# One layer on one core: the fourth and eighth token block's scaling ahead of the memory norms, norm weights on another queue, pooling work spread in the fill

## The chip, the core and the metric

One NeuronCore of a Trainium2 chip runs the whole program. Its engines work side by side and wait for each other through semaphores: TensorE (PE) for matmuls and transposes, VectorE (DVE), ScalarE (ACT), GpSimd (POOL), and SyncE (SP), which here only issues DMAs. The metric is the device time of one execution in microseconds, lower is better.

## The reference

One mixer layer over 1024 tokens of width 1024, in float32:

```python
h = rmsnorm(x, norm_g)
proj = h @ w_in            # pool_v 256 | pool_gate 256 | q, k, v, gate 512 each | mem_q 256 | mem_gate 256
a = pool_mixer(pool_v)     # causal means over 2, 4, 8, 16 tokens minus the token, a 64x64 map per group, a scale
b = stick_breaking_attention(q, k, v)   # 8 heads of 64, strictly causal: sigmoid breaks and their running products
c = memory_attention(mem_q, rmsnorm(mem, mem_norm_g) @ w_mem_kv)  # 4 heads, softmax over 256 memory tokens, q and k normed
out = x + concat(a * silu(pool_gate), b * silu(gate), c * silu(mem_gate)) @ w_out
```

## The kernel before

Every float32 product is made of three faster ones: each operand is split into a high part (`hh`, `wh_*`, written by ACT) and the rest (`hl`, `wl_*`, by DVE or POOL), and PE adds high x high, high x low and low x high. A step of a projection unit `u_*` is these three matmuls of 512 columns for one of eight slices of the width; a unit makes 128 channels in two token halves, so it has 16 steps.

*The beginning.* The two blocks of memory tokens `m[0]`, `m[1]` and the eight of `x` are loaded by SP, with the norm weights as rows of `grow` between them. PE transposes the memory (`m_tr`, tile `tm`) and the norm weights (`gains`, tile `gps`, copied to `gcol` as columns, by which `m_evac` scales what it writes to `mh` and `ml`). The memory's keys and values are accumulated in two banks `kv0`, `kv1` (`kv_step`). A token block is normed in steps of the class `Norm`: `square` (ACT), `root`, `newton` (two 128x1 operations on DVE, three where a column `col` is asked for), `scale` (128x1024, in place, on DVE or POOL). `h_step(th, k)` then transposes slice k of four blocks (tile `tx`) and writes `hh` and `hl`: blocks x0 to x3 are the first half (`th` 0), x4 to x7 the second. The tile x67 holds x6 and x7. `mq_high` and `mq_low` split the weights of the memory queries, whose two units (`u_mq`) run eight slices alternating with `h_step`s; in that loop over k lie also the norms of x4 to x7, the memory's own norms (`mn`, whose result `rm` scales the keys and values) and `kv_evac` (ACT writes `kv` times `rm` to `kvs`). Here the order on DVE, ACT and POOL is that of the code (a manual schedule).

*The attentions.* A list of main steps (scores, transposes, products with the values) and a list `fill` of projection steps are woven by `weave`: it emits fill steps until its model of time says that what the next main step needs is ready. A `Step(pe, fn, occ, lat, needs, gives)` gives that model PE's time, the engines' time and the latency behind it. In the memory attention (`mem_main`) `tr` transposes the weights of 256 tokens to `ta_m`, from which ACT makes `ah_m` and DVE `al_m`, and `av` multiplies both by the memory's values. In the four stick-breaking attentions (two heads each) `ta`, `ah`, `al`, `av` play the same parts; the breaks lie in `be`.

*The pooling.* `pool_parts(r, ...)` gives for channel half r a projection unit `u_pv`, and a list `po[r]`: loading the small map, window sums (`us`, `ps2`, on DVE), means (DVE, then `ph` by ACT and `pl` by POOL), and last two products `py` that are multiplied into the gate `gp`. All but the products cost PE nothing. The lists are inserted into the fill of the last attention at given positions. `ph0` lies in the buffer qb0 and `pl0` in KA0.

*The end.* The mixed channels are multiplied by `w_out` (`oA`, `oS`) in a scheme with fewer products; its weights are loaded into the buffers qa0, qb0, KA0 and others (`quads`, `load_b`), split by `split_b` to `bs`, and the first product (A11) begins behind the last gate's unit `u_mg1`.

Of the kernel before, what the change touches and what calls it, by code (L numbers as in the profile page):

```python
# [14 lines left out]
P = 128  # L15
# [5 lines left out]
HD = 64  # L21
# [4 lines left out]
def layer_kernel(  # L26
# [15 lines left out]
    nc = tc.nc  # L42
# [42 lines left out]
    grow = pool.tile([P, P], F32, tag="pw", name="grow")[0:20, :]  # L85
# [262 lines left out]
    nc.sync.dma_start(grow[8:16, :], mem_norm_g[0].rearrange("(k p) -> k p", p=P))
    nc.sync.dma_start(mt[1][:], mem[0][P : 2 * P, :])
    nc.sync.dma_start(grow[0:8, :], norm_g[0].rearrange("(k p) -> k p", p=P))  # L350
    nc.sync.dma_start(grow[16:18, :], pool_scale[0].rearrange("(k p) -> k p", p=P))
    nc.sync.dma_start(grow[18:19, 0:HD], q_norm_g[0:1, :])
    nc.sync.dma_start(grow[19:20, 0:HD], k_norm_g[0:1, :])
    mn = [Norm(mt[i][:], f"m{i}") for i in range(2)]
    xn = [Norm(xt[i][:], f"x{i}") for i in range(NT)]
    gcol = const.tile([P, 24], F32, name="gcol")
# [8 lines left out]
    def m_tr(i):  # L365
        for kk in range(4):
            for j in range(2):
                k = 2 * kk + j
                nc.tensor.transpose(tm[kk][:, j * M + i * P : j * M + (i + 1) * P], mt[i][:, k * P : (k + 1) * P], ident[:])

    def gains():
        gps = ps("tr", "gps")
        nc.tensor.transpose(gps[:, 0:18], grow[0:18, :], ident[0:18, 0:18])
        nc.tensor.transpose(gps[0:HD, 32:52], grow[:, 0:HD], ident[0:20, 0:20])
        nc.vector.tensor_copy(gcol[:, 0:18], gps[:, 0:18])
# [80 lines left out]
    def kv_newton():  # L456
# [13 lines left out]
        fill=1.0,  # L470
# [102 lines left out]
    def mem_main(mq, ys):  # L573
# [50 lines left out]
        steps = []  # L624
        n = len(items)
        for t in range(n + 4):
            if t < n:
                steps.append(Step(0.44, lambda it=items[t]: qk(it), 1.5, 2.5, [("q", t - 3)], ("q", t)))
            if 0 <= t - 3 < n:
                steps.append(Step(0.43, lambda it=items[t - 3]: tr(it), 0.7 if t < n else 2.2, 2.4, [("q", t - 3)], ("t", t - 3)))  # L630
            if 0 <= t - 4 < n:
                steps.append(Step(0.44, lambda it=items[t - 4]: av(it), 0.3, 0.0, [("t", t - 4)]))
        return steps
# [176 lines left out]
    mn[0].square()  # L810
    mn[1].square()
    m_tr(0)
    gains()
    m_tr(1)
    warm(kvp[1], 4)
    m_evac(0)
    kv_split(0)
# [18 lines left out]
    xn[2].root(True)  # L836
    kv_step(3)
    xn[2].newton()
    xn[3].square()
    xn[3].root(True)  # L840
    xn[2].scale(nc.vector)
    raw_mq = [load_raw(w_in_v[:, :, 2560 + pr * P : 2560 + (pr + 1) * P], f"mq{pr}", early_raw[4 + pr]) for pr in range(2)]
    for i in range(4, 8):
        nc.sync.dma_start(xt[i][:], xv[i * P : (i + 1) * P, :])
# [9 lines left out]
    def mq_low(pr, c, eng):  # L854
        wh, wl = w_mq[pr]
        eng.tensor_tensor(wl[:, c], raw_mq[pr][:, c], f(wh[:, c]), op=ALU.subtract)

    mq_high(0, wc[0])
    mq_low(0, wc[0], nc.gpsimd)
    mq_high(0, wc[1])  # L860
    mq_high(1, wc[0])
    mq_low(1, wc[0], nc.gpsimd)
# [27 lines left out]
    for k in range(KD):  # L890
        half[0, 0][k][1]()
        half[1, 0][k][1]()
        if k + 3 < KD:
            h_step(0, k + 3)
        if k >= 5:
            h_step(1, k - 5)
        if k == 1:
            for i in range(2):
                mn[i].root()
        if k == 3:  # L900
            for i in range(2):
                mn[i].newton(col=rm[:, i : i + 1])
        if k <= 3:
            xn[4 + k].newton()
        if k < 2:
            xn[6 + k].square()
            xn[6 + k].root()
        if k <= 3:
            xn[4 + k].scale(nc.gpsimd if k < 2 else nc.vector)
        if k == 3:  # L910
            u_q[0].weights()
        if k == 4:
            kv_evac()

    plan = {-1:((0, 0), (0, 1), (0, 2)), 0: ((0, 3), (0, 4)), 1: ((1, 0), (1, 1),(1, 2)), 2: ((1, 3),), 3: ((1, 4),)}
# [44 lines left out]
    gm, u_gm = zip(*[gate_unit(2816 + pr * P, f"mg{pr}", "be", lambda pr=pr: y_mem[pr], (("pj", "pj"), ("tr", "av"))[pr]) for pr in range(2)])  # L960
    u_pv, po = zip(*[pool_parts(r, gp[r]) for r in range(2)])
    weave(attn(2), chain([u_q[3], u_k[3], u_v[3]]+[u_g[3]], u_pv[1]), 4, 1.0)
    fill = chain([u_pv[1], u_gp[1], u_pv[0], u_gp[0]]+[u_gm[0]], u_gm[1])
    for r, at in ((0, 46), (1, 22)):
        for n, st in enumerate(po[r][:-2]):
            fill.insert(at + 2 * n, st)
    at = 70 + len(po[0]) + len(po[1]) - 4
    fill[at:at] = po[0][-2:-1]
    fill[at + 6 : at + 6] = po[0][-1:]
    at = 44 + len(po[1]) - 2  # L970
    fill[at:at] = po[1][-2:-1]
# [106 lines left out]
    w1 = split_b("B11", b1)  # L1078
    t1 = quads("KA0")
    load_b(t1, 0, 1)  # L1080
    run(u_gm[1].steps[:8])
    split_a("A11", raw[0, 0])
    s3 = quads("V0")
    tt("S3r", s3, raw[0, 0], raw[1, 0], ALU.subtract)
# [93 lines left out]
```

## Time and profile before

| | us |
|---|---|
| median of 3 runs | 524.44 (523.58 to 524.48) |
| the profiled execution | 524.41 |
| its span, first to last instruction | 522.6 |
| PE busy | 509.8 |
| DVE busy | 392.4 |
| ACT busy | 289.8 |
| POOL busy | 166.4 |

In a row of the view in order of time stand the start and the duration in us, the engine, the line, the operation, the tile written and the tiles read (without their numbers), the shapes and the count; in brackets how long the engine had been idle and what ended that. SPq rows are DMAs being issued. Overlapping rows of one engine are pipelined. In the view of waits stand the total in us, how often, and the longest.

### The profile page before, as it was taken

To read this page: it belongs to the slowest core of one execution; us is meant where nothing else is said; L and a number is where in the kernel's file an instruction comes from. 1 tells how busy PE (TensorE), PEld (TensorE's weight loads), DVE (VectorE), ACT (ScalarE), POOL (GpSimd) and SP (SyncE) were. 2 spreads that over 40 slices of the span, in tenths; PEclk is the share of its full clock that TensorE was granted. 3 is DMA by queue.
4 is the path that set the end of the run, shared out by engine and by line. 5 is a ranking of instruction groups with operands and counts; after the bars stand their busy time and mean duration, and the time that the engine had idled before them with its cause. 6 is when DMAs were issued, how large, how long until landed. Compare 5 with 4: busy or idle time off the path is not lost.

```text
span 522.6 us, 7475 instructions
## 1 busy us (share of the span) xinstructions
PE 509.8 (98%) x2724; PEld 429.3 (82%) x2724; DVE 392.4 (75%) x635; ACT 289.8 (55%) x562; POOL 166.4 (32%) x190
## 2 busy tenths in 40 slices
PE   7889999999999999999999999999999999999997
PEld 6678888888888888888888888888788888888886
DVE  4776777777487876877748776748988769999973
ACT  6887657677555654645545655445535539452400
POOL 4480335244212112202201220122436910044890
PEclk9999999999999999999999999999999999999999
DMA  8911021310111131033101122110110525513033
GB/s 298 349 44 41 7 76 43 80 41 0 41 40 42 42 80 41 0 82 80 42 1 40 41 69 54 40 42 7 35 41 0 162 64 180 163 39 135 26 118 124
DMA packets 37244, 37.25 MB, mean 71 GB/s; under 512 B 1990, under 2 KB 26840, under 8 KB 37208
## 3 DMA queue, kind: packets, MB, share of 16 engines
q1 hardware_dynamic: 37208, 36.78, 22.6%
q8 instruction: 21, 0.34, 0.3%
q14 instruction: 15, 0.12, 0.1%
HBM read 28.39 MB, written 4.19 MB: 62 GB/s over the span
## 4 chain that ended last, share of the span: by engine, by line
PE 85%; DVE 6%; ACT 5%; DMA 2%; issue 1%; ACTq 0%; DVEq 0%
PE av L525 8%; PE z L653 7%; PE ta L506 6%; PE u_g L221 6%; PE u_q L221 6%; PE u_v L221 5%; PE u_k L221 5%; PE u_g L218 3%; PE u_mg L221 3%; PE oS L1060 3%; PE u_q L218 3%; PE oS L1062 3%; PE u_pv L221 3%; PE oS L1061 3%; PE u_v L218 3%; PE u_k L218 2%
## 5 line engine op out<-in xcount | busy, mean ns | idle before, releaser
L661 DVE TENSOR_TENSOR_SCAN be<-be,later 128x128 f32<-128x128 f32 (+3 forms) x64 | 92.0, 1452 | 15.8 <-ACT be L657 14.8
L511 ACT ACTIVATE ah<-ta,mone 128x512 fp32r<-128x512 f32 (+1 forms) x80 | 51.6, 645 | 55.7 <-PE ta L506 54.9
L512 DVE SCALAR_TENSOR_TENSOR al<-ta,ah 128x512 fp32r<-128x512 f32 (+1 forms) x80 | 50.6, 632 | 23.3 <-ACT ah L511 22.2
L657 ACT ACTIVATE be<-z 128x128 f32<-128x128 f32 (+3 forms) x96 | 45.6, 490 | 32.4 <-PE z L653 30.8
L506 PE MATMUL ta<-ident,be 128*128 128x128 f32 x288 | 44.9, 273 | 0.0
L506 PEld LDWEIGHTS ta<-ident,be 128*128 128x128 f32 x288 | 34.8, 140 | 7.6 <-DVE be L661 0.6
L525 PEld LDWEIGHTS av<-ah,V_v 128*128 128x128 f32 x160 | 29.7, 188 | 6.7
L525 PE MATMUL av<-al,V_v 128*128 128x256 f32 (+1 forms) x160 | 31.8, 280 | 1.1 <-DVE al L512 1.1
L525 PE MATMUL av<-ah,V_v 128*128 128x256 f32 (+1 forms) x160 | 30.3, 271 | 0.0
L218 PE MATMUL u_g<-hh,wh_g 128*128 128x512 f32 x64 | 27.5, 430 | 0.0
L218 PE MATMUL u_v<-hh,wh_v 128*128 128x512 f32 x64 | 27.3, 426 | 0.0
L164 POOL TENSOR_TENSOR wl_k<-wr_k,wh_k 128x256 fp32r<-128x256 f32 x16 | 12.0, 782 | 45.6 <-ACT wh_k L160 45.6
L218 PE MATMUL u_k<-hh,wh_k 128*128 128x512 f32 x64 | 26.5, 415 | 0.0
L164 POOL TENSOR_TENSOR wl_g<-wr_g,wh_g 128x256 fp32r<-128x256 f32 x16 | 11.3, 742 | 46.4 <-ACT wh_g L160 31.4
L608 POOL TENSOR_SCALAR pe_m<-pe_m,nb_m 128x256 f32<-128x256 f32 x16 | 16.8, 1047 | 29.0 <-DVE nb_m L605 22.4
L1060 PE MATMUL oS<-bs,hh 128*128 128x512 f32 (+1 forms) x68 | 25.9, 381 | 0.0
L1062 PE MATMUL oS<-bs,hl 128*128 128x512 f32 (+1 forms) x68 | 25.8, 379 | 0.0
L1061 PE MATMUL oS<-bs,hh 128*128 128x512 f32 (+1 forms) x68 | 25.6, 377 | 0.0
L221 PE MATMUL u_v<-hl,wh_v 128*128 128x512 f32 x64 | 25.3, 396 | 0.0
L221 PE MATMUL u_g<-hl,wh_g 128*128 128x512 f32 x64 | 25.3, 395 | 0.0
L221 PE MATMUL u_k<-hl,wh_k 128*128 128x512 f32 x64 | 25.3, 395 | 0.0
L221 PE MATMUL u_k<-hh,wl_k 128*128 128x512 f32 x64 | 25.3, 395 | 0.0
(316 smaller groups left out, 1472.1 us busy)
## 6 DMA issues: line engine op xcount, KB each, us to landing
x<-in_x_dram SPq DMA_DIRECT2D x8, 512.0 KB, 6.4
wr_q<-in_w_in_dram SPq DMA_DIRECT2D x4, 512.0 KB, 3.8
wr_k<-in_w_in_dram SPq DMA_DIRECT2D x4, 512.0 KB, 3.6
wr_v<-in_w_in_dram SPq DMA_DIRECT2D x4, 512.0 KB
KA_k<-KA_k SPq DMA_DIRECT2D x8, 256.0 KB, 5.2
KB_k<-KB_k SPq DMA_DIRECT2D x8, 256.0 KB, 4.6
wr_g<-in_w_in_dram SPq DMA_DIRECT2D x4, 512.0 KB, 4.7
xr<-in_x_dram SPq DMA_DIRECT2D x8, 256.0 KB, 3.3
```

Of the source, the lines that this page charges most:

```text
L218: nc.tensor.matmul(pt[:], wh[:, kc], hh[k][:, c], start=(k == 0), stop=False)
L221: nc.tensor.matmul(pt[:], w[:, kc], h[k][:, c], start=False, stop=(k == KD - 1 and n == 1))
L506: nc.tensor.transpose(tp[:, o : o + P], src, ident[:])
L511: nc.scalar.activation(ah[:, :w], tp[:, :w], AF.Identity, bias=mone[:, 0:1])
L512: nc.vector.scalar_tensor_tensor(al[:, :w], tp[:, :w], -1.0, f(ah[:, :w]), op0=ALU.add, op1=ALU.subtract)
L525: nc.tensor.matmul(av[:, 256 - bw : 256], vs[n], part[:, o : o + bw], start=(first and part is ah and n == 0), stop=(last and part is al a ...
L653: nc.tensor.matmul(zp[:, 0:w], q[h][:, tcol], k[h][:, n, s0 : s0 + w], start=(n == 0), stop=(n == 1))
L657: nc.scalar.activation(be[:, s0 : s0 + w], zp[:, 0:w], AF.Sigmoid, scale=-(HD**-0.5))
L661: nc.vector.tensor_tensor_scan(be[:, rev], be[:, rev], mask, 1.0, op0=ALU.mult, op1=ALU.max)
L1060: nc.tensor.matmul(bk[:, c], xh[:, tcol], wh[:, c], start=(n == 0), stop=False)
L1061: nc.tensor.matmul(bk[:, c], xh[:, tcol], wl[:, c], start=False, stop=False)
L1062: nc.tensor.matmul(bk[:, c], xl[:, tcol], wh[:, c], start=False, stop=(n == 3))
```

## The change

Five loads of norm weights are issued by ACT and not by SP; the transposes of the norm weights stand behind those of the second memory block; x2 is scaled ahead of x3's squares; the first quarter of the memory queries' low weights is formed by DVE and not POOL; the memory's newtons and `kv_evac` move from k = 3 and 4 to k = 5; the latency behind `tr` in the memory attention is 2.8 in place of 2.4; in the last attention the first memory gate's unit stands ahead of the first pooling half's, the pooling's steps stand at other positions of the fill, and the last two products of half 0 lie within the last gate's unit.

```diff
--- before.py
+++ after.py
@@ -345,12 +345,12 @@
     xt += [x67[:, 0:1024], x67[:, 1024:2048]]
     mt = [slot(f"Y{i}", f"m{i}") for i in range(2)]
     nc.sync.dma_start(mt[0][:], mem[0][0:P, :])
-    nc.sync.dma_start(grow[8:16, :], mem_norm_g[0].rearrange("(k p) -> k p", p=P))
+    nc.scalar.dma_start(grow[8:16, :], mem_norm_g[0].rearrange("(k p) -> k p", p=P))
     nc.sync.dma_start(mt[1][:], mem[0][P : 2 * P, :])
-    nc.sync.dma_start(grow[0:8, :], norm_g[0].rearrange("(k p) -> k p", p=P))
-    nc.sync.dma_start(grow[16:18, :], pool_scale[0].rearrange("(k p) -> k p", p=P))
-    nc.sync.dma_start(grow[18:19, 0:HD], q_norm_g[0:1, :])
-    nc.sync.dma_start(grow[19:20, 0:HD], k_norm_g[0:1, :])
+    nc.scalar.dma_start(grow[0:8, :], norm_g[0].rearrange("(k p) -> k p", p=P))
+    nc.scalar.dma_start(grow[16:18, :], pool_scale[0].rearrange("(k p) -> k p", p=P))
+    nc.scalar.dma_start(grow[18:19, 0:HD], q_norm_g[0:1, :])
+    nc.scalar.dma_start(grow[19:20, 0:HD], k_norm_g[0:1, :])
     mn = [Norm(mt[i][:], f"m{i}") for i in range(2)]
     xn = [Norm(xt[i][:], f"x{i}") for i in range(NT)]
     gcol = const.tile([P, 24], F32, name="gcol")
@@ -627,7 +627,7 @@
             if t < n:
                 steps.append(Step(0.44, lambda it=items[t]: qk(it), 1.5, 2.5, [("q", t - 3)], ("q", t)))
             if 0 <= t - 3 < n:
-                steps.append(Step(0.43, lambda it=items[t - 3]: tr(it), 0.7 if t < n else 2.2, 2.4, [("q", t - 3)], ("t", t - 3)))
+                steps.append(Step(0.43, lambda it=items[t - 3]: tr(it), 0.7 if t < n else 2.2, 2.8, [("q", t - 3)], ("t", t - 3)))
             if 0 <= t - 4 < n:
                 steps.append(Step(0.44, lambda it=items[t - 4]: av(it), 0.3, 0.0, [("t", t - 4)]))
         return steps
@@ -810,8 +810,8 @@
     mn[0].square()
     mn[1].square()
     m_tr(0)
+    m_tr(1)
     gains()
-    m_tr(1)
     warm(kvp[1], 4)
     m_evac(0)
     kv_split(0)
@@ -836,9 +836,9 @@
     xn[2].root(True)
     kv_step(3)
     xn[2].newton()
+    xn[2].scale(nc.vector)
     xn[3].square()
     xn[3].root(True)
-    xn[2].scale(nc.vector)
     raw_mq = [load_raw(w_in_v[:, :, 2560 + pr * P : 2560 + (pr + 1) * P], f"mq{pr}", early_raw[4 + pr]) for pr in range(2)]
     for i in range(4, 8):
         nc.sync.dma_start(xt[i][:], xv[i * P : (i + 1) * P, :])
@@ -856,7 +856,7 @@
         eng.tensor_tensor(wl[:, c], raw_mq[pr][:, c], f(wh[:, c]), op=ALU.subtract)
 
     mq_high(0, wc[0])
-    mq_low(0, wc[0], nc.gpsimd)
+    mq_low(0, wc[0], nc.vector)
     mq_high(0, wc[1])
     mq_high(1, wc[0])
     mq_low(1, wc[0], nc.gpsimd)
@@ -897,7 +897,7 @@
         if k == 1:
             for i in range(2):
                 mn[i].root()
-        if k == 3:
+        if k == 5:
             for i in range(2):
                 mn[i].newton(col=rm[:, i : i + 1])
         if k <= 3:
@@ -909,7 +909,7 @@
             xn[4 + k].scale(nc.gpsimd if k < 2 else nc.vector)
         if k == 3:
             u_q[0].weights()
-        if k == 4:
+        if k == 5:
             kv_evac()
 
     plan = {-1:((0, 0), (0, 1), (0, 2)), 0: ((0, 3), (0, 4)), 1: ((1, 0), (1, 1),(1, 2)), 2: ((1, 3),), 3: ((1, 4),)}
@@ -960,16 +960,13 @@
     gm, u_gm = zip(*[gate_unit(2816 + pr * P, f"mg{pr}", "be", lambda pr=pr: y_mem[pr], (("pj", "pj"), ("tr", "av"))[pr]) for pr in range(2)])
     u_pv, po = zip(*[pool_parts(r, gp[r]) for r in range(2)])
     weave(attn(2), chain([u_q[3], u_k[3], u_v[3]]+[u_g[3]], u_pv[1]), 4, 1.0)
-    fill = chain([u_pv[1], u_gp[1], u_pv[0], u_gp[0]]+[u_gm[0]], u_gm[1])
-    for r, at in ((0, 46), (1, 22)):
-        for n, st in enumerate(po[r][:-2]):
-            fill.insert(at + 2 * n, st)
-    at = 70 + len(po[0]) + len(po[1]) - 4
-    fill[at:at] = po[0][-2:-1]
-    fill[at + 6 : at + 6] = po[0][-1:]
-    at = 44 + len(po[1]) - 2
-    fill[at:at] = po[1][-2:-1]
-    fill[at + 6 : at + 6] = po[1][-1:]
+
+    fill = chain([u_pv[1], u_gp[1], u_gm[0], u_pv[0], u_gp[0]], u_gm[1])
+    spread = [(18 + 2 * n, st) for n, st in enumerate(po[1][:-2])]
+    spread += [(46, po[1][-2]), (50, po[1][-1])]
+    spread += [(65 + (3 * n) // 2, st) for n, st in enumerate(po[0][:-2])]
+    for at, st in sorted(spread, key=lambda e: -e[0]):
+        fill.insert(at, st)
     weave(attn(3), fill, 6, 3.0)
 
 
@@ -1078,7 +1075,10 @@
     w1 = split_b("B11", b1)
     t1 = quads("KA0")
     load_b(t1, 0, 1)
-    run(u_gm[1].steps[:8])
+    run(u_gm[1].steps[:4])
+    run(po[0][-2:-1])
+    run(u_gm[1].steps[4:8])
+    run(po[0][-1:])
     split_a("A11", raw[0, 0])
     s3 = quads("V0")
     tt("S3r", s3, raw[0, 0], raw[1, 0], ALU.subtract)
```

DVE at the third and fourth token block, before (a name's last number is its place in the program):

```order
L140 TENSOR_SCALAR ss_x2_119<-ss_x2_119 128x1
L133 TENSOR_SCALAR ss_x3_120<-ss_x3_120 128x1
L145 TENSOR_SCALAR x2_102<-x2_102,ss_x2_119 128x1024
L139 TENSOR_SCALAR ss_x3_120<-ss_x3_120 128x1
L140 TENSOR_SCALAR ss_x3_120<-ss_x3_120 128x1
L145 TENSOR_SCALAR x3_103<-x3_103,ss_x3_120 128x512
L395 SCALAR_TENSOR_TENSOR hl0_91<-tx0_0_350,gcol_125,hh0_83 128x512
L145 TENSOR_SCALAR x3_103<-x3_103,ss_x3_120 128x512
L395 SCALAR_TENSOR_TENSOR hl1_92<-tx0_1_359,gcol_125,hh1_84 128x512
L395 SCALAR_TENSOR_TENSOR hl2_93<-tx0_2_366,gcol_125,hh2_85 128x512
```

and after:

```order
L140 TENSOR_SCALAR ss_x2_119<-ss_x2_119 128x1
L145 TENSOR_SCALAR x2_102<-x2_102,ss_x2_119 128x1024
L133 TENSOR_SCALAR ss_x3_120<-ss_x3_120 128x1
L139 TENSOR_SCALAR ss_x3_120<-ss_x3_120 128x1
L140 TENSOR_SCALAR ss_x3_120<-ss_x3_120 128x1
L145 TENSOR_SCALAR x3_103<-x3_103,ss_x3_120 128x512
L856 TENSOR_TENSOR wl_mq0_342<-raw0_132,wh_mq0_341 128x512
L395 SCALAR_TENSOR_TENSOR hl0_91<-tx0_0_350,gcol_125,hh0_83 128x512
L145 TENSOR_SCALAR x3_103<-x3_103,ss_x3_120 128x512
L395 SCALAR_TENSOR_TENSOR hl1_92<-tx0_1_359,gcol_125,hh1_84 128x512
```

x2's scaling stands one row earlier, and the subtraction of line 856 stands between the two halves of x3's scaling; on POOL it is gone.

DVE at the eighth block, before:

```order
L395 SCALAR_TENSOR_TENSOR hl6_97<-tx0_6_451,gcol_125,hh6_89 128x512
L139 TENSOR_SCALAR ss_m0_115<-ss_m0_115 128x1
L140 TENSOR_SCALAR ss_m0_115<-ss_m0_115 128x1
L142 TENSOR_TENSOR rm_74<-ss_m0_115 128x1
L139 TENSOR_SCALAR ss_m1_116<-ss_m1_116 128x1
L140 TENSOR_SCALAR ss_m1_116<-ss_m1_116 128x1
L142 TENSOR_TENSOR rm_74<-ss_m1_116 128x1
L139 TENSOR_SCALAR ss_x7_124<-ss_x7_124 128x1
L140 TENSOR_SCALAR ss_x7_124<-ss_x7_124 128x1
L145 TENSOR_SCALAR x67_99<-x67_99,ss_x7_124 128x1024
L395 SCALAR_TENSOR_TENSOR hl7_98<-tx0_7_481,gcol_125,hh7_90 128x512
L395 SCALAR_TENSOR_TENSOR hl0_91<-tx1_0_497,gcol_125,hh0_83 128x512
```

and after:

```order
L395 SCALAR_TENSOR_TENSOR hl6_97<-tx0_6_451,gcol_125,hh6_89 128x512
L139 TENSOR_SCALAR ss_x7_124<-ss_x7_124 128x1
L140 TENSOR_SCALAR ss_x7_124<-ss_x7_124 128x1
L145 TENSOR_SCALAR x67_99<-x67_99,ss_x7_124 128x1024
L395 SCALAR_TENSOR_TENSOR hl7_98<-tx0_7_475,gcol_125,hh7_90 128x512
L395 SCALAR_TENSOR_TENSOR hl0_91<-tx1_0_488,gcol_125,hh0_83 128x512
L139 TENSOR_SCALAR ss_m0_115<-ss_m0_115 128x1
L140 TENSOR_SCALAR ss_m0_115<-ss_m0_115 128x1
L142 TENSOR_TENSOR rm_74<-ss_m0_115 128x1
L139 TENSOR_SCALAR ss_m1_116<-ss_m1_116 128x1
L140 TENSOR_SCALAR ss_m1_116<-ss_m1_116 128x1
L142 TENSOR_TENSOR rm_74<-ss_m1_116 128x1
```

The memory norms' six rows have moved from between `hl6` and x7's newton to behind the second half's `hl0`.

PE in the memory attention, before:

```order
L218 MATMUL u_v0_0_999<-hh3_86,wh_v0_811 128x512
L221 MATMUL u_v0_0_999<-hl3_94,wh_v0_811 128x512
L221 MATMUL u_v0_0_999<-hh3_86,wl_v0_812 128x512
L525 MATMUL av_3_1052<-ah_m0_1_0_995,vm_616 128x256 x2
L525 MATMUL av_3_1052<-al_m0_1_0_996,vm_616 128x256 x2
L218 MATMUL u_v0_0_999<-hh4_87,wh_v0_811 128x512
L221 MATMUL u_v0_0_999<-hl4_95,wh_v0_811 128x512
L221 MATMUL u_v0_0_999<-hh4_87,wl_v0_812 128x512
```

and after:

```order
L218 MATMUL u_v0_0_999<-hh3_86,wh_v0_811 128x512
L221 MATMUL u_v0_0_999<-hl3_94,wh_v0_811 128x512
L221 MATMUL u_v0_0_999<-hh3_86,wl_v0_812 128x512
L218 MATMUL u_v0_0_999<-hh4_87,wh_v0_811 128x512
L221 MATMUL u_v0_0_999<-hl4_95,wh_v0_811 128x512
L221 MATMUL u_v0_0_999<-hh4_87,wl_v0_812 128x512
L525 MATMUL av_3_1055<-ah_m0_1_0_995,vm_616 128x256 x2
L525 MATMUL av_3_1055<-al_m0_1_0_996,vm_616 128x256 x2
```

One step of `u_v0` has moved ahead of `av_3`; the same happens with a step of `u_k0` at `av_1`.

In the last attention DVE forms `al_3_1_1_0` (line 512) ahead of two of the pooling's operations (lines 763 and 766, on `us1`) that stood directly ahead of it before. The products `py0_0` and `py0_1` (lines 781 to 783), which stood within the attention, now stand behind the fourth and the eighth of the sixteen steps of `u_mg1`, and so do the last reads of `ph0` and `pl0`.

## The prediction

> **What bounds the kernel now.** I read the busy times of the page first, then the clock, then the waits of TensorE.
>
> ```profile
> span 522.6 us, 7475 instructions
> PE 509.8 (98%) x2724; PEld 429.3 (82%) x2724; DVE 392.4 (75%) x635; ACT 289.8 (55%) x562; POOL 166.4 (32%) x190
> PEclk9999999999999999999999999999999999999999
> ```
>
> TensorE (PE) works for 509.8 of 522.6 us at an undisturbed clock, and the change removes no matmul. So all that can be won lies in the 12.8 us in which PE does not work, and anything that does not shorten or lengthen a wait of PE costs nothing. The view of waits, for PE alone, says where they are (us in total, times, longest):
>
> ```profile
> PE tx L392 <- DVE x L145: 3.3, 2, 1.8
> PE tm L363 <- POOL bones L94: 2.3, 1, 2.3
> PE av L525 <- DVE al_m L517: 1.3, 2, 1.1
> PE av L525 <- DVE al L512: 1.1, 1, 1.1
> ...
> ```
>
> These four sum to 8.0 us; what else there is lies mostly at the start and in the tail behind the last matmul. The change leaves the 2.3 us at the start alone and aims at rows one, three and four. I take each wait as the excess of the distance between two starts of matmuls over the usual distance, because that is what a shorter wait gives back.
>
> **Fourth token block (x3).** In time order, with the instruction that each idle engine waited for in brackets:
>
> ```profile
> 21.11 0.81 DVE L145 TENSOR_SCALAR x<-x,ss_x 128x1024 f32<-128x1024 f32 x1
> 22.21 1.26 POOL L856 TENSOR_TENSOR wl_mq<-raw,wh_mq 128x512 fp32r<-128x512 f32 x1 [2.49 <-ACT wh_mq L852]
> 22.33 1.42 DVE L145 TENSOR_SCALAR x<-x,ss_x 128x512 f32<-128x512 f32 x1
> 22.56 0.61 ACT L852 ACTIVATE wh_mq<-wr_mq 128x512 fp32r<-128x512 f32 x1
> 23.81 1.20 PE L392 MATMUL tx<-ident,x 128*128 128x128 f32 x9 [1.50 <-DVE x L145]
> 24.18 0.69 ACT L394 ACTIVATE hh<-tx,gcol 128x512 fp32r<-128x512 f32 x1 [1.01 <-PE tx L392]
> ```
>
> The scaling of half of x3 took 1.42 us, though twice the elements took 0.81 at 21.11. It ended at 23.75, 0.28 after POOL's subtraction (23.47): the two did not share, DVE stood until POOL was done. The Trainium skill ("SBUF — State Buffer", section "SBUF: two separate sides") says why: DVE and GpSimd share a port pair as an exclusive lock, held for the whole instruction. The trace agrees here; the rule also speaks against the change, since the subtraction that comes to DVE has two SBUF inputs and so can be locked out itself.
>
> The change gives this subtraction to DVE, behind the scaling, so nothing runs on POOL at 22.3. The scaling then takes about half of 0.81, 0.4 us, and starts about 0.1 earlier (a 0.15 us operation steps behind x2's scaling): x3 is ready near 22.7 instead of 23.75. Full gain 1.0 us. ACT is the next limit: hh can't start before ACT's copy ends at 23.17, but it started at 24.18, so 1.0 is there too. The subtraction on DVE, even at the 1.26 us that POOL took, is done by 24.0, and its result is wanted by the product behind hh, which ends at about 23.9: hidden, or 0.1 late at most. Against this stands the beginning:
>
> ```profile
> 1.16 0.35 SPq L348 DMA_DIRECT2D grow<-in_mem_norm_g_dram  x1
> 3.22 0.40 SPq L149 DMA_DIRECT2D wr_kv<-in_w_mem_kv_dram  x1
> 6.69 1.06 ACT L123 ACTIVATE sq_m<-m 128x1024 f32<-128x1024 f32 x1 [1.46 <-DMA m<-in_mem_dram]
> 7.18 1.09 PE L369 MATMUL tm<-ident,m 128*128 128x128 f32 x8
> 7.29 0.18 DVE L375 COPY gcol<-gps 128x18 f32<-128x18 f32 x1 [3.22 <-PE gps L374]
> 7.75 0.82 ACT L406 ACTIVATE mh<-tm,gcol 128x256 fp32r<-128x256 f32 x2
> ```
>
> The norm weights' transposes now stand behind the eight of the second memory block. These start when m[1] has landed (6.7) and take about 0.8, so gps comes at 7.5, gcol at 8.0 instead of 7.5, and mh 0.35 later than 7.75. The five weight loads on ACT's queue take five issues off SP (0.35 us for the one at 1.16, and five of them and m[1]'s in the 2.1 us up to 3.22), so the first wr_kv goes out some 1.6 us sooner, and m[1] 0.4. I count nothing for this: every later load also waits for the landing of an earlier one. ACT issues them while it waits for the first memory block. The Trainium skill ("DMA: Bandwidth & Descriptors", section "Issuing engines are not separate DMA queues") holds that a second issuing engine brings no second path, only issue time; this agrees with costing it at nothing. Bounds for the start as a whole: −0.4 (m[1]'s issue) to +0.45 (the full delay of mh). I take +0.25. x3 is then worth 1.05 − 0.25 = **0.8 us**, between 0.5 and 1.1.
>
> **Eighth token block (x7) and the memory norms.**
>
> ```profile
> 34.34 0.74 DVE L395 SCALAR_TENSOR_TENSOR hl<-tx,gcol,hh 128x512 fp32r<-128x512 f32 x1
> 35.00 0.27 DVE L139 TENSOR_SCALAR ss_m<-ss_m 128x1 f32<-128x1 f32 x1
> 35.93 0.49 PE L392 MATMUL tx<-ident,x 128*128 128x128 f32 x3
> 36.82 0.26 DVE L139 TENSOR_SCALAR ss_x<-ss_x 128x1 f32<-128x1 f32 x1
> 37.30 0.81 DVE L145 TENSOR_SCALAR x<-x,ss_x 128x1024 f32<-128x1024 f32 x1
> 38.17 0.33 PE L392 MATMUL tx<-ident,x 128*128 128x128 f32 x1 [1.75 <-DVE x L145]
> ```
>
> PE has three of four transposes by 36.2 and waits to 38.17: 1.97 us. Between hl (ends 35.0) and x7's newton (36.82) DVE spends 1.82 us on the six small operations of the memory norms. With these behind, x7's newton begins at 35.0, its scaling ends at 38.11 − 1.82 = 36.3, and PE would wait 0.1 to 0.2. Everything shifts alike by x3's 0.8. Bounds: all of 1.97; or 0.9, if the scaling meets POOL's weight subtractions and is stretched by the 1.0 that the one at 22.33 lost.
>
> The norms and the two evacuations of the memory keys and values (0.69 each on ACT) then come two steps later, ahead of the second hh and hl of this half on ACT. This delays those by some 0.9 us; what waits is the transposes' PSUM banks (four, reused in turn) and u_q0's bank, which held the first of the memory products. I count 0.2 us of new wait there. x7: **1.6 us**.
>
> **Memory attention.**
>
> ```profile
> 90.72 0.69 DVE L291 TENSOR_TENSOR KB_k<-u_k,KB_k 64x512 fp32r<-64x512 f32 x1
> 91.45 0.69 DVE L517 TENSOR_TENSOR al_m<-ta_m,ah_m 128x512 fp32r<-128x512 f32 x1
> 92.19 0.50 PE L525 MATMUL av<-al_m,vm 128*128 128x256 f32 x2 [1.05 <-DVE al_m L517]
> 92.53 0.40 PE L218 MATMUL u_v<-hh,wh_v 128*128 128x512 f32 x1
> 92.77 0.40 PE L221 MATMUL u_v<-hl,wh_v 128*128 128x512 f32 x1
> ```
>
> al_m stands on DVE behind the keys' KA_k and KB_k, which the change leaves there; PE waits 1.22 us for it. The latency figure 2.8 for 2.4 sets one u_v0_0 step between: three matmuls of 0.235 us spacing (92.53, 92.77), **0.7 us** of work inside the wait. The other half of this row of the waits (0.37 us, near 111) stays. Bounds 0 and 0.7.
>
> **Pooling over twice the steps.**
>
> ```profile
> 369.98 0.17 DVE L763 TENSOR_TENSOR us<-ps,cnt 64x16 f32<-64x16 f32 x1
> 370.07 0.73 DVE L766 SCALAR_TENSOR_TENSOR us<-ps,cnt,us 64x496 f32<-64x496 f32 x1
> 370.84 0.69 DVE L512 SCALAR_TENSOR_TENSOR al<-ta,ah 128x512 fp32r<-128x512 f32 x1
> 371.59 0.51 PE L525 MATMUL av<-al,V_v 128*128 128x256 f32 x2 [1.07 <-DVE al L512]
> ```
>
> Here al stands behind two operations of the pooling, 370.84 − 369.98 = 0.86 us; now it is ahead of them. The wait of 1.24 shrinks to about 0.4: **0.86 us**. Bounds 0 and 1.24. Elsewhere in this attention there is no wait to win, only some to make: the deadlines of al grow tight where the first channel half's pooling now runs (some 404 to 430 us). PE shows no wait there now and DVE is not full:
>
> ```profile
> 360.00:425.00 65.00, 63.93 (x346) 53.71 (x345) 54.71 (x75) 33.60 (x60) 38.00 (x29) 1.00 0.16 49
> 425.00:505.00 80.00, 80.00 (x353) 65.43 (x353) 73.62 (x106) 37.34 (x65) 30.90 (x21) 1.00 0.34 112
> ```
>
> (columns behind the length: PE, PEld, DVE, ACT, POOL busy, then clock, DMA share, GB/s.) DVE has 10.3 us free of 65 there, 6.4 of 80 after.
>
> The pooling's last products (py0) move into the last memory gate, the second ends near 435.5 by the old clock. They hold the buffers into which the last weights are loaded:
>
> ```profile
> 427.20 0.84 SPq L1014 DMA_DIRECT2D b_qb<-in_w_out_dram  x2
> DMA to landing us min/median/max: 3.2/4.3/5.3
> 443.38 1.28 DVE L1030 TENSOR_TENSOR bs<-b_qb,bs 128x512 fp32r<-128x512 f32 x2
> 441.94 0.40 PE L1060 MATMUL oA<-bs,hh 128*128 128x512 f32 x1
> ```
>
> The loads slip by 8.5 us, to 435.7. With 4.3 to 5.3 us (the view of b_qb, third row) b_qb lands by 441. b_KA's four follow on the same queue from 436.6; at the same 5.3 us the first lands by 442, and DVE's differences of it stand ahead of the splits of b_qb, so these end near 444.6. PE begins the last product at 441.94 and needs the third of its four weight pieces after 24 matmuls, at 447.5. About 2.9 us remain, so I count nothing; if that cover were gone, each us beyond it would be a us of time.
>
> **Sum.** 0.8 + 1.6 + 0.7 + 0.86 = 3.96 us. The profiled execution took 524.41 us (span 522.6), the runs' median is 524.44, so the same subtraction holds for both: 524.4 − 4.0 = **520.4 us**.
>
> **Rivals.**
> (a) Partial: the three early gains come, but the later attention gives its own back. The g_mg0 gate now takes a buffer of the breaks; the last block's breaks can be formed only when it is done, by my estimate 3 us ahead of their transposes, and DVE's tightest al has some 0.2 us. For it: DVE at 84% from 360 to 425. Against: no wait of PE there now. A give-back of 1 to 2 us on 520.4: 521.3 to 522.6.
> (b) The pooling and the latency figure do nothing: al is delayed by another operation, the new step pushes av_3's successors. Without 0.86 and 0.7: 522.0. x7's scaling stretched by POOL (0.7 lost) instead of these: 521.1; with one of them, 521.9.
> (c) The other side: the late weight loads. If the splits of b_qb end later than 447.5, that is over 12 us behind the last py0 instead of 9, PE stands, and DVE, with 6.4 us free in 80, carries the delay into the next products. For it: loads 8.5 us later in the stage where DMA share is highest after the start (0.34). Against: DMA is busy only a third of the time. It cancels the gain at 4 us of wait; with 5 it gives 525.4.
> (d) Better: the waits at x3 and x7 vanish wholly, m[1] lands earlier: 1.1 + 1.97 + 0.7 + 1.24 = 5.0, so 519.4.
>
> **How the numbers follow.** My forecast (519.9 to 521.2) 0.50; (a) 0.17; (b) 0.13; (c) 0.10, of which 0.06 ends above the old time by more than 0.2% and 0.04 about it; (d) 0.06; something small in all parts that eats the gain to within 0.2% 0.04. 0.2% or 1.05 us is about what a measurement of this kernel can tell from no change, so faster means below 523.4. Faster 0.84 (with 0.02 of the tail of (a) falling to no change), same 0.10, slower 0.06. The range runs from (d)'s 519.2 to 523.0, past (b) and (a)'s far end (522.6); the likeliest case's own range is 519.9 to 521.2.
>
> **What the profile after would show.** In PE's waits: the row tx behind x at 0.5 us or less in total; al_m near 0.8; al near 0.4 or gone; no new row in 425 to 505. The half scaling of x3 at 0.4 to 0.5 us. DVE's x7 newton right behind hl. If a row of oA or oS behind bs or b_qb appears, (c) is right; if ta behind be appears near 400, (a). The prediction is wrong if the waits are gone and the time stays: then they reappear later under other names.

## The result and the profile after

The changed kernel is slower: 527.57 us (527.16 to 530.78, six runs) against 524.16 (523.58 to 524.48, six runs of the kernel before), a ratio of 1.0077 with a 95% interval of [1.0053, 1.0101], as brackets behind a ratio are throughout. One slow run of e1 below, of 1789 us, is not in its ratio. The prediction was 520.4. The profiled execution took 527.43 us. First lines of its page:

```profile
span 525.7 us, 7471 instructions
PE 511.5 (97%) x2724; PEld 429.5 (82%) x2724; DVE 393.8 (75%) x636; ACT 289.2 (55%) x562; POOL 162.0 (31%) x189
```

PE does the same 2724 matmuls; the span is 3.1 us longer. The view of waits for PE (us in total, times, longest):

```profile
PE av L525 <- DVE al L512: 2.8, 1, 2.8
PE tm L363 <- POOL bones L94: 2.3, 1, 2.3
PE z L653 <- ACT be L657: 1.3, 1, 1.3
PE av L525 <- DVE al_m L517: 1.3, 2, 0.9
PE kv L425 <- ACT wh_kv L169: 1.1, 1, 1.1
PE tx L392 <- DVE x L145: 0.9, 1, 0.9
PE ta L506 <- DVE be L661: 0.5, 1, 0.5
...
```

The row tx went from 3.3 to 0.9, as meant. But a wait for al of 2.8 us stands on top, z behind be and ta behind be are new, and al_m stayed at 1.3. Where the time went shows in the starts of the same matmul in both traces, after minus before:

| matmul | before | after | difference | this stretch | predicted |
|---|---|---|---|---|---|
| first product of the memory's keys | 9.14 | 9.41 | +0.27 | +0.27 | +0.25 |
| first transpose of x | 21.63 | 21.74 | +0.11 | −0.16 | 0 |
| transpose behind x3 | 24.63 | 23.95 | −0.68 | −0.79 | −1.05 |
| first query step (behind x7) | 42.37 | 40.06 | −2.31 | −1.63 | −1.6 |
| first memory score | 71.39 | 69.70 | −1.69 | +0.62 | 0 |
| 36th memory score (behind av_3) | 97.07 | 94.69 | −2.38 | −0.69 | −0.7 |
| 49th memory score | 112.28 | 110.58 | −1.70 | +0.68 | 0 |
| first pooling step | 344.60 | 342.93 | −1.67 | +0.03 | 0 |
| first product oA | 441.94 | 444.97 | +3.03 | +4.70 | −0.86 |
| last product oS | 519.17 | 522.19 | +3.02 | 0 | 0 |

Up to 343 us the kernel is 1.7 us ahead. Then the last attention loses 4.7, where 0.86 was to be won. By the excess of distances: 0.98 won at 371 (1.24 to 0.26), 1.44 lost at z (374), 0.53 at ta (378), 0.31 near 419, 3.01 at av (428); about 0.4 is spread over the rest.

**428 us.** ACT, POOL, DVE and PE in order of time (lines between left out):

```profile
422.21 0.69 ACT L511 ACTIVATE ah<-ta,mone 128x512 fp32r<-128x512 f32 x1
...
422.53 3.76 POOL L1033 TENSOR_TENSOR b_V<-g_g 128x512 f32<-128x512 f32 x3
...
425.10 1.73 DVE L1033 TENSOR_TENSOR g_g<-g_g,y_mem 128x512 f32<-128x512 f32 x1 [2.48 <-POOL b_V L1033]
426.76 0.68 DVE L334 TENSOR_TENSOR gp<-u_pg,gp 128x512 f32<-128x512 f32 x1
427.36 1.14 DVE L512 SCALAR_TENSOR_TENSOR al<-ta,ah 128x512 fp32r<-128x512 f32 x2
428.09 0.50 PE L525 MATMUL av<-al,V_v 128*128 128x256 f32 x2 [2.85 <-DVE al L512]
```

Line 1033 is the helper `tt` of the last product: `tt("S1r", raw[1, 0], raw[1, 0], raw[1, 1], ALU.add)` adds the memory's mixed channels to a gate in place. DVE stands 2.48 us because POOL still reads what the addition overwrites (three differences of its own, S3r, of g_g into b_V); the addition begins when POOL is through two of the three. al stands behind it in DVE's queue though its input, the ah of 422.21, is done at 422.9. With the first memory gate's unit now ahead of the first pooling half's, the memory's channels y_mem0 have been multiplied by their gate at 397.9 (435.0 before), and the scheduler sets the addition between two of the last al. In the kernel before it came behind the attention and took 0.68 and not 1.73:

```profile
457.21 0.68 DVE L1036 TENSOR_TENSOR g_g<-g_g,y_mem 128x512 f32<-128x512 f32 x1
```

DVE's order in the changed program reads:

```
L512 SCALAR_TENSOR_TENSOR al_3_1_3_1_4374<-ta_3_1_3_1_4368,ah_3_1_3_1_4373 128x512
L1033 TENSOR_TENSOR g_g1_2122<-g_g1_2122,y_mem0_818 128x512
L334 TENSOR_TENSOR gp_3884<-u_pg0_0_4285,gp_3884 128x512
L512 SCALAR_TENSOR_TENSOR al_3_1_3_2_4397<-ta_3_1_3_2_4391,ah_3_1_3_2_4396 128x512
```

**374 to 378 us.** The same view there:

```profile
369.01 1.84 DVE L766 SCALAR_TENSOR_TENSOR us<-ps,cnt,us 64x496 f32<-64x496 f32 x1
369.03 1.28 POOL L770 TENSOR_TENSOR pl<-ps,ph 64x512 fp32r<-64x512 f32 x1 [6.55 <-ACT ph L769]
...
372.27 0.63 ACT L769 ACTIVATE ph<-us 64x512 fp32r<-64x512 f32 x1 [1.54 <-DVE us L764]
...
373.04 0.63 ACT L769 ACTIVATE ph<-ps 64x512 fp32r<-64x512 f32 x1
...
373.58 0.57 ACT L657 ACTIVATE be<-z 128x512 f32<-128x512 f32 x1
...
374.20 0.74 PE L653 MATMUL z<-KB_k,qb_q 128*128 128x512 f32 x2 [1.28 <-ACT be L657]
...
374.88 5.16 DVE L661 TENSOR_TENSOR_SCAN be<-be,later 128x768 f32<-128x768 f32 x2
```

al went ahead as meant, which puts the pooling's L766 0.69 us (one al) later, and there it meets POOL's subtraction L770: 1.84 us where it took 0.73 at 370.07 before. Everything behind it on DVE is late. ACT has two ph ahead of be, as it had before, and PE gets be 1.28 us late. The two scans of be that follow take 5.16 us beside two more subtractions of POOL; that is not new, for in the kernel before they read:

```profile
375.46 5.15 DVE L661 TENSOR_TENSOR_SCAN be<-be,later 128x768 f32<-128x768 f32 x2
```

They only come too late for PE now.

**The beginning.** x3 and x7, and behind them the place where 0.62 is lost:

```profile
22.53 0.55 DVE L145 TENSOR_SCALAR x<-x,ss_x 128x512 f32<-128x512 f32 x1
...
23.00 0.68 DVE L856 TENSOR_TENSOR wl_mq<-raw,wh_mq 128x512 fp32r<-128x512 f32 x1
...
34.34 0.26 DVE L139 TENSOR_SCALAR ss_x<-ss_x 128x1 f32<-128x1 f32 x1
34.64 0.15 DVE L140 TENSOR_SCALAR ss_x<-ss_x 128x1 f32<-128x1 f32 x1
34.83 0.98 DVE L145 TENSOR_SCALAR x<-x,ss_x 128x1024 f32<-128x1024 f32 x1
...
38.78 1.27 ACT L439 ACTIVATE kvs<-kv,rm 128x512 f32<-128x512 f32 x2 [1.86 <-DVE rm L142]
...
39.94 1.27 ACT L394 ACTIVATE hh<-tx,gcol 128x512 fp32r<-128x512 f32 x2
...
41.08 0.59 ACT L268 ACTIVATE G_mq<-u_mq 64x512 fp32r<-64x512 f32 x1
...
60.92 3.98 DVE L494 SCALAR_TENSOR_TENSOR km<-tk,gcol,km 64x256 fp32r<-64x256 f32 x8 [1.36 <-ACT km L489]
64.93 0.17 DVE L566 COPY ssb<-sp 128x8 f32<-128x8 f32 x1
...
65.24 1.02 PE L564 MATMUL sp<-bones,sqq 128*128 128x2 f32 x8 [0.38 <-DVE ssb L566]
```

The scaling of half of x3 takes 0.55 and not 1.42, and x7's newton stands right behind hl. The eight km operations of the memory's keys came only 1.68 us earlier (62.60 before), less than PE's 2.31, and PE waits for the copy ssb behind them. This lag shows from 41 us on: there ACT's first G_mq comes 1.72 us earlier than before, which was:

```profile
42.80 0.58 ACT L268 ACTIVATE G_mq<-u_mq 64x512 fp32r<-64x512 f32 x1
```

Ahead of it ACT is busy without a gap from 38.78 on, with the two moved evacuations `kvs` and the hh behind them. DVE waits for ACT's hh there, then works nearly without a gap, and keeps these 1.7 us up to km. The rows suggest that the moved evacuations cost the 0.6; no run here moves x7's scaling and leaves them in the old place.

### The profile page after: what moved, and what is told of

Read it like the earlier page. It is cut to its first block, busy times and chain, and to the rows that moved or that the text cites. A ratio compares the mean times of both kernels' runs of the same rounds, so it can differ in the third digit from the quotient of the medians.

```text
span 525.7 us, 7471 instructions
## 1 busy us (share of the span) xinstructions
PE 511.5 (97%) x2724; PEld 429.5 (82%) x2724; DVE 393.8 (75%) x636; ACT 289.2 (55%) x562; POOL 162.0 (31%) x189
## 4 chain that ended last, share of the span: by engine, by line
PE 79%; DVE 12%; ACT 6%; POOL 2%; issue 2%; ACTq 0%; DVEq 0%; POOLq 0%
PE av L525 7%; PE z L653 6%; PE u_g L221 6%; PE ta L506 5%; PE u_v L221 5%; PE u_k L221 5%; PE u_q L221 4%; PE u_g L218 3%; PE oS L1057 3%; PE oS L1059 3%; PE oS L1058 3%; PE u_pv L221 3%; PE u_mg L221 3%; PE u_v L218 2%; PE u_k L218 2%; PE u_q L218 2%
## 5 line engine op out<-in xcount | busy, mean ns | idle before, releaser
L661 DVE TENSOR_TENSOR_SCAN be<-be,later 128x128 f32<-128x128 f32 (+3 forms) x64 | 90.2, 1424 | 16.6 <-ACT be L657 15.7
L525 PEld LDWEIGHTS av<-al,V_v 128*128 128x128 f32 x160 | 24.2, 189 | 3.7 <-DVE al L512 3.7
L653 PE MATMUL z<-KB_k,qb_q 128*128 128x512 f32 (+3 forms) x96 | 25.2, 351 | 1.4 <-ACT be L657 1.3
L597 ACT ACTIVATE pe_m<-z_m,nb_m,qsc 128x256 f32<-128x256 f32 x32 | 17.8, 561 | 15.2 <-DVE nb_m L593 15.1
```

The source lines that it names most:

```text
L525: nc.tensor.matmul(av[:, 256 - bw : 256], vs[n], part[:, o : o + bw], start=(first and part is ah and n == 0), stop=(last and part is al a ...
L653: nc.tensor.matmul(zp[:, 0:w], q[h][:, tcol], k[h][:, n, s0 : s0 + w], start=(n == 0), stop=(n == 1))
L661: nc.vector.tensor_tensor_scan(be[:, rev], be[:, rev], mask, 1.0, op0=ALU.mult, op1=ALU.max)
```

## The experiments

The theory from the profile after: the loss is two waits behind what stands ahead in an in-order queue (the addition at 428; the pooling meeting POOL at 369). Rivals: the pooling's new positions are bad as such ("phase"), or DVE is full.

**S1r behind the attention** (e1): the changed kernel, with this edit.

```diff
     weave(attn(3), fill, 6, 3.0)
+    attn_end = next(i for i in reversed(nc.cur_bb.bb.instructions) if i.engine == mybir.EngineType.DVE)
...
-    tt("S1r", raw[1, 0], raw[1, 0], raw[1, 1], ALU.add)
+    with tc.issue_after(attn_end):
+        tt("S1r", raw[1, 0], raw[1, 0], raw[1, 1], ALU.add)
```

> The changed kernel, with the four additions S1r (line 1033, which overwrite halves of g_g0 to gp1) queued on DVE behind the last attention. Theory 'queue place': in the changed kernel the second of them stands on DVE ahead of al_3_1_3_2 and waits there for POOL, which still reads the same half (S3r); PE's wait of 2.85 us at 428 is this wait. Then the time falls by about 3 us, 527.6 to 524.6, and no wait of PE behind al over 0.5 us is left after 400. Rival 'DVE is full': DVE, slowed by POOL's four differences on the shared port, can't form al in time whatever stands in the queue; then at most the 1.7 us of the one addition come back, the time is 526 or more and a wait of PE behind al over 1 us stays.

524.62 against 524.28, ratio 1.0006 [0.9997, 1.0015]. The wait of 2.8 is gone:

```profile
...
PE z L653 <- ACT be L657: 1.3, 1, 1.3
PE av L525 <- DVE al_m L517: 1.3, 2, 0.9
...
PE av L525 <- DVE al L512: 0.2, 1, 0.2
```

It comes later now (457.74) and nothing new waits for it, so its place alone cost 3 us: shown.

**The pooling part alone** (e2): the kernel before with the new `fill`, `spread` and `u_gm[1]` pieces.

```diff
-    fill = chain([u_pv[1], u_gp[1], u_pv[0], u_gp[0]]+[u_gm[0]], u_gm[1])
+    fill = chain([u_pv[1], u_gp[1], u_gm[0], u_pv[0], u_gp[0]], u_gm[1])
+    spread = [(18 + 2 * n, st) for n, st in enumerate(po[1][:-2])]
...
```

> The kernel before with only the pooling's new places and the new order of the last attention's fill. Theory 'the pooling costs it all': from the two traces the waits from 363 us on grew by 4.5 us net (0.96 won at 371, 2.0 lost at 374 to 378, 3.4 at 420 to 430, the rest small), so 524.2 + 4.5 = 528.7. Rival 'phase': the new waits arise because PE comes 1.7 us earlier there while DVE does not; without the early gains they shrink by as much, 527.0 or less.

530.62, ratio 1.0121 [1.0105, 1.0136]: 6.3 us. The waits at z, ta and av are those of the changed kernel although nothing ahead of 343 us was shifted, so the "phase" rival fell. The time is about 2 us more than expected, and these lie behind the wait at 428. PE's rows, and the windows (columns as in the prediction's: length, PE, PEld, DVE, ACT, POOL, clock, DMA share, GB/s):

```profile
429.65 0.50 PE L525 MATMUL av<-al,V_v 128*128 128x256 f32 x2 [2.88 <-DVE al L512]
...
431.08 0.63 PE L218 MATMUL u_pg<-hh,wh_pg 128*128 128x512 f32 x1
431.51 0.63 PE L221 MATMUL u_pg<-hl,wh_pg 128*128 128x512 f32 x1
```

```profile
427.00:430.00 3.00, 0.35 (x3) 0.35 (x4) 3.00 (x4) 0.00 (x0) 2.52 (x2) 1.00 0.00 0
430.18:433.60 3.42, 3.42 (x9) 2.65 (x8) 0.00 (x0) 0.00 (x0) 0.00 (x0) 0.50 0.00 0
434.00:436.00 2.00, 2.00 (x11) 1.63 (x11) 1.21 (x3) 0.88 (x2) 0.00 (x0) 1.00 0.00 0
```

Behind a wait of 2.88 us the granted clock is 0.50 for 3.42 us, and matmuls of 512 columns stand 0.43 apart and not 0.235. Half of 3.42 is 1.7 us of lost work. All four runs of this kernel have the lower mean clock (0.996 to 0.997). Of the changed kernel's six runs four have clock 1.000 and 527.16 to 527.62 us, two have 0.997 and 528.56, 0.994 and 530.78; only a run at 1.000 has a trace.

**S1r behind, in the pooling part alone** (e7): e2 with the edit of e1.

> As e2_pool_only, with S1r queued behind the attention as in e1_s1r_behind. In e2_pool_only PE waited 2.88 us at 429.65 and then ran nine matmuls at 0.427 us spacing instead of 0.235, its granted clock 0.55 to 0.60 from 430 to 434. Theory 'the wait costs the clock': both go with the wait, 3.0 + 1.8 us less than 530.6, so 525.8, and the granted clock stays at 1.00 from 425 to 440. Rival 'another cause of the clock': only the wait goes, 527.6, with the clock still under 0.7 somewhere after 430.

526.05, ratio 1.0032 [1.002, 1.0044]: 4.6 us less than e2 (both beside 524.3 before), of which 2.9 is the wait and 1.7 the clock, which stays at 1.00 from 424 to 440. That the wait brings the lower clock in this kernel is shown. The pooling part without the addition still costs 1.8 us.

**The beginning alone** (e3): the kernel before with the first half of the diff (norm weights, x2, wl_mq, memory newtons, `kv_evac`), latency 2.4 and the old pooling.

> The kernel before with only the changes up to the memory's norms (loads on ACT's queue, order of transposes, x2's scaling, the subtraction on DVE, newtons and kv_evac at k = 5), latency 2.4 and pooling as before. Theory 'gains stay up to 1.7': 2.3 us won at x3 and x7, 0.6 lost again at 65 us behind the norms of the memory queries; nothing later takes the rest: 524.2 - 1.7 = 522.5. Rival 'it is all given back': DVE's chain through the memory attention sets the time, 523.8 to 524.5.

523.05, ratio 0.9975 [0.9965, 0.9984]: 1.2 us won.

**The latency figure alone** (e4): 2.8 for 2.4 in `tr`'s step.

> The kernel before with only the latency 2.8 in place of 2.4 in the memory attention. Theory 'moved wait': 0.7 us is won at av_3 and lost at av_8, since DVE's chain of the memory attention is as long as before: 524.2, within 0.2. Rival, the prediction's: 0.7 won and kept, 523.5.

524.31, ratio 1.0001 [0.9993, 1.001]. The excess at av_3 fell from 1.22 to 0.52 and that at av_8 rose from 0.37 to 1.07: the wait moved and nothing was won. The rows at av_8, here of the changed kernel, where it did the same:

```profile
108.21 0.67 DVE L310 TENSOR_TENSOR vt_v<-vt_v,u_v 128x512 f32<-128x512 f32 x1
108.81 0.68 DVE L517 TENSOR_TENSOR al_m<-ta_m,ah_m 128x512 fp32r<-128x512 f32 x1
...
109.54 0.51 PE L525 MATMUL av<-al_m,vm 128*128 128x256 f32 x2 [0.90 <-DVE al_m L517]
```

al_m stands behind vt of the one u_v0 step that was put between.

**No subtraction on POOL** (e5): e1 with the low part of the pooled second channel half (`pl1`, the one that is pooled first) set to zero, so that part of the product is left out.

```diff
-            (nc.gpsimd if [1, 1][r] else nc.vector).tensor_tensor(pl[rows, c], dst[rows, c], f(ph[rows, c]), op=ALU.subtract)
+            if r == 1:
+                nc.gpsimd.memset(f(pl[rows, c]), 0.0)
+            else:
+                nc.gpsimd.tensor_tensor(pl[rows, c], dst[rows, c], f(ph[rows, c]), op=ALU.subtract)
```

> As e1_s1r_behind, but POOL's four subtractions for the low part of the pooled second channel half (pl1, line 770) are replaced by a POOL memset to zero: that low part is left out of the result. Theory 'shared port': in e1_s1r_behind the DVE operation of line 766 at 368.3 takes 1.84 us because POOL's subtraction started at the same time; everything behind it on DVE and ACT is 1.1 us late, and so are the breaks whose score bank PE waits for (1.28 us at 373.5). Without the subtraction line 766 takes 0.75, PE's wait behind be falls to 0.3 or less, and the time falls by 1.0 to 1.5 us, to 523.4. Rival 'queue order': the wait comes from the two ph on ACT ahead of be and from al ahead of line 766 on DVE; then PE's wait stays above 1.0 and the time within 0.4 of 524.6.

522.25, ratio 0.9961 [0.9949, 0.9973], 2.4 us below e1, more than expected. The same two DVE rows as at 369.01 and 374.88 above:

```profile
368.47 0.73 DVE L766 SCALAR_TENSOR_TENSOR us<-ps,cnt,us 64x496 f32<-64x496 f32 x1
...
372.95 3.14 DVE L661 TENSOR_TENSOR_SCAN be<-be,later 128x768 f32<-128x768 f32 x2
```

1.84 became 0.73, 5.16 became 3.14, and the wait of z fell from 1.3 to 0.2. That POOL's subtractions stretch DVE's work here, and that this makes the wait at 374, is shown: of the four only the first is over when that be begins. The wait of ta at 378 is gone too, but there the faster scans have a share, and these gain what the change had not cost, since the kernel before has 5.15. That can be why e5 won more than expected; how much each gave is not separated.

**The subtraction on DVE** (e6): e1 with `[1, 0][r]` in that line.

> As e1_s1r_behind, with the same four subtractions (pl1) on DVE instead of POOL, nothing left out. By 'shared port' line 766 takes 0.75 us again, but DVE has 4 x 0.7 us more to do in the same stretch, two of them ahead of the next breaks' scan: 524.3, between 523.5 and 525.3. By 'queue order' it is only more work in the queue: 525.3 or more.

523.71, ratio 0.999 [0.9982, 0.9999]. The waits of z and ta are gone, but av waits 0.5 for ah and 0.2 for al near 380: about 0.9 us below e1, not a place without cost.

**The pooling's operations pinned** (e8): e3 with the second channel half's multiplications, means and ph kept in the order of the code.

```diff
+            pin = tc.keep_in_program_order if r == 1 else (lambda i: i)
...
-            nc.scalar.activation(ph[rows, c], dst[rows, c], AF.Copy)
+            pin(nc.scalar.activation(ph[rows, c], dst[rows, c], AF.Copy))
```

> As e3_begin_only (pooling as before), with the mean steps of the pooling's second channel half on DVE and ACT held in the order of the code: al_3_1_1_0 then stands ahead of them on DVE, and the breaks be of the next scores ahead of ph on ACT. Theory 'order on both queues': the 1.25 us at 371 come back without a new wait behind be: 523.05 - 1.0 = 522.0. Rival 'DVE is full there': the work that is held back meets the next scans and al, another wait of about 1 us appears between 375 and 395, and the time stays at 523.0.

523.88, ratio 0.9994 [0.9983, 1.0005]. The wait at 371 is gone and none came at 374, but a new one stands at 393.6:

```profile
PE py L782 <- DVE gp L785: 2.0, 1, 2.0
```

```profile
389.61 0.72 DVE L767 SCALAR_TENSOR_TENSOR ps<-us,cnt 64x496 f32<-64x496 f32 x1
...
390.86 2.02 DVE L661 TENSOR_TENSOR_SCAN be<-be,later 128x896 f32<-128x896 f32 x1
392.80 0.73 DVE L785 SCALAR_TENSOR_TENSOR gp<-py,gcol,gp 128x512 f32<-128x512 f32 x1
```

The rival's wait came, twice as long as expected, and the time is 0.8 us above e3's and not the same. DVE works 36.2 of the 40 us from 360 to 400, but 36.1 in e3, which has no wait there, so its load does not tell the two apart. Its order does: the means that were held back now stand ahead of a scan of 2.0 us, and this ahead of the gp that PE waits for. Two of the twelve executions have a mean clock of 0.996 and take 525.73 and 525.93 us; neither has a trace.

**Pinned, products five steps later** (e10): e8 with `at = 49` for 44.

> As e8_pinned, with the two products py1 five steps later in the fill. In e8_pinned the wait behind al at 371 was gone and no new one behind be came, but py1_0 waited 2.0 us at 393 for the low part that POOL forms from the held back means. Theory 'only the place of py1': five steps are 3.5 us of matmuls ahead of it, the 2.1 us come back: 523.9 - 2.0 = 521.9, faster than both kernels. Rival 'DVE is full': the first half's pooling, whose buffers py1 holds, is late in turn and PE waits elsewhere between 395 and 430: 523 or more.

524.01, ratio 1.0 [0.9991, 1.0009]. The expectation fell: the 2.0 us became 1.4 (u_pg behind gp, 394) and 0.6 (al, 410). It had also taken the wait in e8 for one on POOL's low part; the row above names DVE's gp, and POOL had ended its last subtraction ahead of it at 386.0.

**The norm weights alone** (e11): the kernel before with the five loads on ACT's queue and `gains()` behind `m_tr(1)`.

> The kernel before with only the norm weights' part of the change: their five loads on ACT's queue, their transposes behind the second memory block. Theory 'it costs': e9_no_norm, without it, ran at 522.3 where e3_begin_only ran at 523.05; in the traces PE's first product of the keys waited 1.28 us for ACT with it and 0.60 without, since gcol comes later. So 524.2 + 0.5 to 0.7 = 524.7 to 524.9. Rival 'noise of the landings': the first loads land up to 0.7 us earlier or later from run to run, and the two were timed on other days of the chip: 524.2, within 0.2.

524.49 against 523.94, ratio 1.0012 [1.0003, 1.0021]: it costs, as the theory had it.

**The beginning without the norm weights** (e9): e3 with the loads on SP and `gains()` between the two `m_tr`.

> As e3_begin_only, but the norm weights' loads stay on SP and their transposes ahead of the second memory block, as in the kernel before. It tells what those two parts are worth. Theory 'the start costs little': the sum of PE's waits up to 20 us was 5.1 to 5.5 us with them and 4.5 to 5.4 without, which differs as much between runs of one order: within 0.4 us of e3_begin_only (522.7 to 523.5). Rival, the prediction's: they delay the first products by 0.25 and x3 with them, 522.8 at once. Rival 'SP's queue': the earlier issue of the big loads brings x0 to x3 sooner, so without it 523.8 or more.

522.30 against 524.09, ratio 0.9967 [0.9955, 0.998], below all three expectations. The first products' wait behind wh_kv is 0.4, against 1.1 in e3, e11 and the changed kernel. Both comparisons, each kernel beside its own runs of the kernel before, give the norm weights' part the same price, about +0.55 us; e11's interval is 0.2 to 1.1.

**al first** (e12): e9, with al and al_m given priority over what is ready beside them.

```diff
+            with tc.high_priority(100):
+                nc.vector.tensor_tensor(al[:, :w], tp[:, :w], f(ah[:, :w]), op=ALU.subtract)
```

> As e9_no_norm, with a higher priority for al and al_m: in the memory attention al_m0_1_0 then stands ahead of KB_k on DVE, and several other al_m ahead of small operations of the softmax; PE's order stays. Theory 'DVE's chain is as long': the wait of 1.2 us at av_3 shrinks by 0.7, what is put off (KB_k, the softmax's reciprocals) makes av_8's wait or another one as much longer: 522.3, within 0.3. Rival 'place in the queue': the 0.7 us are kept, 521.6 or less.

521.34 against 523.94, ratio 0.9948 [0.9935, 0.9962]: the fastest version, 2.6 us ahead of the kernel before. The expectation was wrong. In time order, the place of av_3:

```profile
88.37 0.67 DVE L519 TENSOR_TENSOR al_m<-ta_m,ah_m 128x512 fp32r<-128x512 f32 x1
89.08 0.69 DVE L291 TENSOR_TENSOR KB_k<-u_k,KB_k 64x512 fp32r<-64x512 f32 x1
...
89.10 0.50 PE L527 MATMUL av<-al_m,vm 128*128 128x256 f32 x2 [0.21 <-DVE al_m L519]
```

al_m stands ahead of KB_k, the row al_m of the waits falls from 1.3 to 0.2, and PE's order is unchanged. That wait was not DVE's load but its order. The wait of 1.2 us for al near 369 stays: there al still stands behind the pooling's two operations.

## Why the prediction was wrong

- *Pooling, 0.86 with bounds 0 and 1.24.* The step that failed is "Elsewhere in this attention there is no wait to win, only some to make", followed by a bound of 0 below and by the busy share of DVE as the evidence. The win at 371 came (0.98), but the bound below had to go far under nothing. A wait in an in-order queue needs no full engine: DVE stood idle for 2.48 us ahead of the addition that held up al. DVE's order behind the moved unit follows from the program alone, and the prediction read it only at the pooling. What the runs showed in place of the 0.86: the addition there cost 2.9 to 3.0 (e7, e1), and the pooling part as a whole 6.3 (e2).
- *What al delays.* The prediction put al ahead of L763 and L766 and did not ask what they would meet 0.69 us later, though it had found the same stretching at x3. The Trainium skill ("SBUF — State Buffer", section "SBUF: two separate sides") names the shared pair as a lock that the operation which starts first keeps; the trace agrees on the stretch, 0.73 to 1.84, and leaves open who was first: DVE's record begins 0.02 us ahead of POOL's (369.01, 369.03), and yet it is DVE that lasts 1.1 us longer. Price of the place: 1.44 at z, and 0.53 at ta, where the cause is argued and not separated.
- *Memory attention, 0.7.* The gain at av_3 came (0.69). "The other half of this row stays" failed: it grew by 0.68, since the step put between brings its own vt ahead of the next al_m. Alone the edit is worth 0.0.
- *The beginning.* x7 gave 1.63 where 1.6 was predicted. x3 gave 0.79 of 1.05: the scaling took 0.55 and not 0.4, and began no earlier, as three small operations of x3 now follow x2's scaling. The start cost about 0.55 in the paired runs, not 0.25; the interval, 0.2 to 1.1, holds both that and the upper bound of 0.45. The 0.2 counted for the memory's norms and evacuations was the term that was too small: it looked at the waits right behind them, while the 0.62 were lost near 65 us, where ACT's and DVE's chain had not moved as far as PE. Together e3 gave 1.2 where 0.8 + 1.6 = 2.4 stood.
- *Rivals.* (a) had the right stage and the sign, and breaks were late (0.5 at ta, 378), but behind POOL's stretch and not behind the buffer of g_mg0 at the last block; its size (1 to 2 us) was too small. (c) foretold the right side by loads that were never late: no wait of oA or oS is in the list after. (b), half right on the latency figure, fell on the pooling. (d)'s own sum gives 519.4, where the range begins at 519.2.
- *The sum.* e3 (−1.2), e4 (0.0) and e2 (+6.3) make +5.1; the change as a whole gives +3.4. Four runs of six have a clock of 1.000, where e2's four all have the drop; without its 1.7 the sum is +3.4. That they agree to the tenth is luck: each part's interval is about 1 us wide or more.

What stays open: whether the moved evacuations alone hold back the km chain; whether the lower clock in two of the changed kernel's six runs comes from its wait of 2.85 us, and if so, why only there; and how much of the 0.53 at 378 is POOL's.

## What to carry to other kernels

After a unit is moved, read each engine's order up to the end of the program, and look for an in-place operation that has become ready early: it can stand in front of critical work while another engine still reads what it overwrites. A wait of PE behind an engine that is not full is first a question of order; putting the short operation that PE waits for ahead won about a microsecond (e12 beside e9) where moving PE's work only moved the wait (e4). When one operation is pulled forward, ask what the ones behind it will now meet.

## What was not expected of the hardware

A single wait of 2.88 us halved the clock for 3.42 us, at a cost of 1.7 us beyond the wait. The Trainium skill ("TensorE: Matmul & The Clock Gate", section "Part 1: The HAM clock gate (the "warmup" mystery)") gives an idle window of about 3.4 us and 426.7 ns between cold matmuls of 512 columns, and says that the window is free-running: the 0.43 us agrees, but here 2.88 us were enough in four runs of four, and of the changed kernel, whose wait was 2.85 us in the trace, two runs of six have a lower mean clock. Two DVE scans of 128x768 and 128x640 take 3.14 us without (e5) and 5.16 us beside POOL's subtractions of 64x512, a price that the kernel before pays too.
